# Stick-breaking attention in a two-layer decoder trunk: another order of units, masks, read-outs and conversions

## The chip, the cores and the metric

The kernel runs on one core of one Trainium2 chip. The metric is device time in microseconds: the median of 3 runs is 1889.95 us (1888.29 to 1889.99). The profile comes from one further execution.

## The reference, cut to what matters

Two layers work on 512 tokens of width 2048, in fp32. The first is a sparse attention layer and isn't touched. The second is stick-breaking attention over keys and values of 4 groups, with 16 query heads of 128 (4 heads to a group):

```python
z = einsum('bqngd,bsnd->bngqs', qg, k) * HEAD_DIM ** -0.5
strict = key_pos[None, :] < t[:, None]
log_om = where(strict, -softplus(z), 0.0)
suffix = cumsum(log_om, reverse=True) - log_om       # over the keys
a = where(strict, exp(log_sigmoid(z) + suffix), 0.0)
o = einsum('bngqs,bsnd->bqngd', a, v)
...
return (o * silu(gate)) @ w_o                         # gate = x @ w_in[:, WIDTH_B:]
```

So each query sums softplus over the keys between a key and itself, from the latest key backwards, and the sum has to go from one block of 128 keys to the next earlier one.

## The kernel before, in words

All matrices are laid out features by tokens, in tiles of 128 by 512. Every fp32 product is three fp32r matmuls (mm3, L135 to L138) of high and low halves; `split` (L131 to L133) makes the halves: a copy on ACT (hi) and a subtraction on DVE (lo). The weights come through SP's DMA queue, and each 128 x 512 piece is split into wh and wl (`plain_items`, L232).

**The stage.** For each of 4 head groups g (loop at L1357) PE computes the gate projection for 4 blocks of 128 columns into banks 0 to 3 (64 steps of one mm3, `gemm_w`, L289; for group 0 `gate_first`, L1214), and between its steps the attention of the group in 10 units. A unit (i, kb) is query block i (4 heads x 128 queries = 512 columns) against key block kb <= i (128 rows). The class `Sticks` (L1240) has its steps:

- `logits` (L1252): mm3 of keys and queries into a bank z (4 + u % 2; bank 7 for unit 0). On a diagonal unit (kb == i) DVE adds the mask (z<-z,gone). ACT does Abs (wk<-z), Exp and Ln (wk<-wk); DVE joins max(z, 0) and the logarithm into softplus (wk<-z,wk): "the sum" in the prediction.
- `parts` (L1268): for kb < i DVE adds the total that the later key block left (wk<-wk,t or wk<-t,ident,wk); DVE makes the halves sh and sl. For kb > 0 ACT copies a row or 32 rows of z into a tile t.
- `weights` (L1287): two matmuls (L1291) of a triangle of -1 with sh and sl onto z; ACT takes the exponential (wk<-z); for kb > 0 DVE subtracts z from t (t<-t,z), which is the total for unit (i, kb - 1): "the read-out". Then the halves of the result, hi on ACT and lo on DVE (c<-wk).
- `values` (L1303): three matmuls (L1310 to L1312) with the values onto bank 6 or 7 (o); after a row's last unit ACT copies it to F (f<-o).

Units stand in the order of L1244: a row's units run from its diagonal to kb = 0, always two places apart, so the total has a turn's time. The diagonals are units 0, 1, 7 and 8.

**The order.** `turn` (L1321) for s = 1 to 11 issues on PE: logits of s, one gate step, values of s - 2, one gate step, weights of s - 1, then three gate steps (fewer for some turns of group 0). The rest of `logits` and of `parts` for unit s follows where these are called. PE keeps this order as written. On ACT and DVE the compiler of the kernel schedules by its own model of time (L1432); what runs under `paced` (L325) is held behind the instruction of its engine that was written just before it. A weight conversion is not held so, nor is a SiLU, so a held instruction written right after one of them hangs on that one alone and may move with it.

**Conversions.** Queries lie in F and are scaled and split for each row i by `split_scaled` (L1208: c<-f on ACT and on DVE), into Q[i], once the previous group has finished with row i (L1336: after turns 8, 9 and 11 the rows 2, 3 and 0; L1373: row 1 at the end of the group). `split_keys` (L1164: c<-E) converts a group's keys. They wait in the list `bg`, and `pumped` (L339) takes one from it at each gate step (at every second one in group 0).

**Between groups** (L1370 to L1377): when the gate is done, ACT takes its SiLU from banks 0 to 3 (wk<-g) and DVE multiplies the result into F. The next group then loads ACT's table for Exp and Ln (L1359), issues the logits of units 0 and 1 (`begin`, L1316), and 11 gate steps before turn 1. Group 0 starts beside its own gate (L1345 to L1355).

Of the kernel before, what the change touches and what calls it, by code (L numbers as in the profile page):

```python
# [10 lines left out]
F32 = mybir.dt.float32  # L11
# [66 lines left out]
def trunk_kernel(  # L78
# [85 lines left out]
    units = []  # L164
# [1075 lines left out]
    class Sticks:  # L1240

        units = [(3, 3), (2, 2), (3, 2), (2, 1), (3, 1), (2, 0), (3, 0), (1, 1), (0, 0), (1, 0)]  # L1244

        def __init__(self, g):
# [3 lines left out]
            self.out = {}  # L1250

        def logits(self, u):  # L1252
            i, kb = self.units[u]
            z = bank(4 + u % 2 if u else 7, "z")
            ks = slice(kb * 128, (kb + 1) * 128)
            mm3(z, [k[:, ks] for k in K[self.g]], Q[i], True, True)
            e = work()
            sp = work()
            if kb == i:
                v = z.rearrange("p (h q) -> p h q", h=4)  # L1260
                dve.tensor_tensor(v, v, gone[i % 2].unsqueeze(1).broadcast_to([128, 4, 128]), ALU.add)
            act.activation(e, z, AF.Abs)
            act.activation(e, e, AF.Exp, scale=-1.0)
            act.activation(e, e, AF.Ln, bias=1.0)
            dve.scalar_tensor_tensor(sp, z, 0.0, e, ALU.max, ALU.add)
            self.state[u] = z, sp

        def parts(self, u):  # L1268
# [9 lines left out]
            hi, lo = (px.tile([128, 512], F32R, name=f"s{s}", tag=f"s{s}", bufs=2) for s in "hl")  # L1278
            dve.tensor_copy(hi, sp)
            dve.tensor_tensor(lo, sp, hi.bitcast(F32), ALU.subtract)  # L1280
            if kb:
                rows = slice(96, 128) if kb % 2 else slice(0, 1)
                self.total[i, kb] = px.tile([128, 512], F32, name="t", tag="t", bufs=3)
                act.activation(self.total[i, kb][rows], z[rows], AF.Copy)
            self.state[u] = z, hi, lo

        def weights(self, u):  # L1287
# [6 lines left out]
            if kb:  # L1294

                rows = slice(96, 128) if kb % 2 else slice(0, 1)
                total = self.total[i] = self.total.pop((i, kb))
                dve.tensor_tensor(total[rows], total[rows], z[rows], ALU.subtract)
            hi, lo = A[u % 2]
            split(hi, lo, a)  # L1300
            self.state[u] = hi, lo

        def values(self, u):  # L1303
# [7 lines left out]
            pe.matmul(o, vl, hi, start=False, stop=False)  # L1311
            pe.matmul(o, vh, lo, start=False, stop=kb == 0)  # L1312
            if kb == 0:
                act.activation(F[self.g][:, :, i * 128 : (i + 1) * 128], o.rearrange("p (h q) -> p h q", h=4), AF.Copy)
# [40 lines left out]
    gemm = pumped(chunk, 2)  # L1355

    for g in range(4):  # L1357
        if g:
            log_exp()  # L1359
            banks = mm_banks("g")  # L1360
            gemm = pumped(gemm_w(items, plain, banks))
            sticks = Sticks(g)
            sticks.begin(0)
            sticks.begin(1)
        if 0 < g < 3:
            bg.append(lambda g=g: split_keys(g + 1))
        steps(gemm, 11 if g else 0)
        for s in range(1, 12):
# [67 lines left out]
```

## Time and profile before

| | |
|---|---|
| median of 3 runs | 1889.95 us |
| the profiled execution | 1889.72 us, span 1888.0 us |
| PE, matmuls | 1865.0 us busy (99%), 9181 instructions |
| PEld, weight loads | 1577.3 us (84%) |
| DVE | 1235.1 us (65%) |
| ACT | 938.6 us (50%) |
| DMA | 189.21 MB, mean 100 GB/s |
| the chain that ended last | PE 94%, DVE 3%, ACT 2%, issue 1% |

Times are microseconds from the start of the span. A row of the timeline gives start, duration, engine, line, operation, out<-in by the program's names (buffer numbers left out: c is any of the tiles for halves of keys, queries, values and results), the shape, and in brackets the engine's idle time before it with what ended that. All helpers' instructions have line 111. A matmul of 128 x 512 is shown 0.39 long, but they overlap: what counts is the distance between starts. The four groups lie about at 1240 to 1324, 1391, 1459 and 1511 us.

### The profile page before, as it was taken

The page shows a single profiled execution, that of the slowest core. Times are in us where ns is not written, and L with a number is a line of the kernel's source. Part 1 is how long each engine was busy: PE and PEld are TensorE (multiplying, and loading weights), DVE is VectorE, ACT ScalarE, POOL GpSimd, SP SyncE. Part 2 cuts the span into 40 slices and gives each one's busy share as a digit, 9 for nine tenths or more (in the row PEclk, how much of TensorE's full clock was granted, in tenths as well). Part 3 has the DMA queues.
Part 4 walks back from the last instruction along what each step waited for, and adds up shares of the span by engine and source line. Part 5 has one row for each costly group of instructions (what it writes and reads, how often), then busy time and mean ns, then how long its engine had stood idle before and what let it go on. Part 6 is the DMA issues. An engine that isn't in the chain of part 4 may idle for free.

```text
span 1888.0 us, 24839 instructions
## 1 busy us (share of the span) xinstructions
PE 1865.0 (99%) x9181; PEld 1577.3 (84%) x9181; DVE 1235.1 (65%) x2395; ACT 938.6 (50%) x1696; POOL 4.7 (0%) x20
## 2 busy tenths in 40 slices
PE   9999999999999999999999999998999999999998
PEld 8898888888888888888888999976777788888887
DVE  5768678567565455675377888876877745567534
ACT  3546423455554433474245444477777643347422
POOL 0000000000000000000000000000000000000000
PEclk9999999999999999999999999999999999999999
DMA  6442333312221522433343333322222162242333
GB/s 195 126 123 62 95 101 90 101 56 68 78 67 57 189 90 79 126 98 122 101 146 112 101 102 110 104 78 68 63 62 65 57 189 92 79 131 91 123 101 112
DMA packets 111178, 189.21 MB, mean 100 GB/s; under 512 B 8528, under 2 KB 29008, under 8 KB 111056
## 3 DMA queue, kind: packets, MB, share of 16 engines
q1 hardware_dynamic: 111056, 187.62, 32.8%
q8 instruction: 72, 1.18, 0.3%
q14 instruction: 50, 0.41, 0.1%
HBM read 179.21 MB, written 8.39 MB: 99 GB/s over the span
## 4 chain that ended last, share of the span: by engine, by line
PE 94%; DVE 3%; ACT 2%; issue 1%; DMA 0%; SPq 0%; ACTq 0%; DVEq 0%
PE g L136 11%; PE g L137 11%; PE g L138 11%; PE o L138 7%; PE o L136 7%; PE o L137 7%; PE m L136 4%; PE m L138 4%; PE m L137 4%; PE q L136 3%; PE q L138 3%; PE q L137 3%; PE k L137 2%; PE k L138 2%; PE k L136 2%; ACT wk L111 1%
## 5 line engine op out<-in xcount | busy, mean ns | idle before, releaser
L111 ACT ACTIVATE wh<-raw 128x512 fp32r<-128x512 f32 (+3 forms) x685 | 397.8, 582 | 699.5 <-PE g L137 231.1
L111 DVE TENSOR_TENSOR wl<-raw,wh 128x512 fp32r<-128x512 f32 (+3 forms) x685 | 430.6, 629 | 461.6 <-ACT wh L111 446.2
L136 PE MATMUL g<-xh,wh 128*128 128x512 f32 x1024 | 405.0, 396 | 0.0
L137 PE MATMUL g<-xl,wh 128*128 128x512 f32 x1024 | 400.6, 391 | 0.0
L138 PE MATMUL g<-xh,wl 128*128 128x512 f32 x1024 | 400.6, 391 | 0.0
L138 PEld LDWEIGHTS g<-xh,wl 128*128 128x128 f32 x1024 | 192.9, 188 | 41.4
L137 PEld LDWEIGHTS g<-xl,wh 128*128 128x128 f32 x1024 | 193.2, 189 | 37.5
L136 PEld LDWEIGHTS g<-xh,wh 128*128 128x128 f32 x1024 | 193.1, 189 | 37.3 <-issue 0.3
L138 PE MATMUL o<-xh,wl 128*128 128x512 f32 x512 | 199.3, 389 | 0.0
L136 PE MATMUL o<-xh,wh 128*128 128x512 f32 x512 | 199.2, 389 | 0.0
L137 PE MATMUL o<-xl,wh 128*128 128x512 f32 x512 | 199.2, 389 | 0.0
L138 PEld LDWEIGHTS o<-xh,wl 128*128 128x128 f32 x512 | 96.1, 188 | 20.4 <-DVE wl L111 0.3
L137 PEld LDWEIGHTS o<-xl,wh 128*128 128x128 f32 x512 | 96.1, 188 | 20.0
L136 PEld LDWEIGHTS o<-xh,wh 128*128 128x128 f32 x512 | 96.1, 188 | 19.8
L136 PE MATMUL q<-xh,wh 128*128 128x512 f32 x256 | 99.6, 389 | 0.0
L137 PE MATMUL q<-xl,wh 128*128 128x512 f32 x256 | 99.6, 389 | 0.0
L138 PE MATMUL q<-xh,wl 128*128 128x512 f32 x256 | 99.6, 389 | 0.0
L111 ACT ACTIVATE sh<-st 128x512 fp32r<-128x512 f32 x80 | 49.7, 624 | 44.4 <-DVE st L111 44.3
L111 ACT ACTIVATE wk<-z 128x512 f32<-128x512 f32 x80 | 47.2, 594 | 42.1 <-PE z L138 15.7
L111 DVE TENSOR_TENSOR sl<-st,sh 128x512 fp32r<-128x512 f32 x80 | 55.1, 690 | 13.9 <-ACT sh L111 13.9
L111 DVE TENSOR_TENSOR xl<-f,xh 128x512 fp32r<-128x512 f32 x80 | 54.4, 687 | 12.6 <-ACT f L111 12.3
L138 PEld LDWEIGHTS q<-xh,wl 128*128 128x128 f32 x256 | 48.0, 188 | 10.1
(287 smaller groups left out, 3323.7 us busy)
## 6 DMA issues: line engine op xcount, KB each, us to landing
raw<-w_in_a SPq DMA_DIRECT2D x95, 512.0 KB, 3.7
raw<-w_in_b SPq DMA_DIRECT2D x64, 512.0 KB, 3.8
raw<-w_ple_gate SPq DMA_DIRECT2D x52, 512.0 KB, 3.7
raw<-w_o_a SPq DMA_DIRECT2D x24, 512.0 KB, 3.7
raw<-w_o_b SPq DMA_DIRECT2D x24, 512.0 KB, 3.8
raw<-w_kv_b SPq DMA_DIRECT2D x16, 512.0 KB, 3.8
raw<-w_ple_gate SPq DMA_DIRECT2D x24, 256.0 KB, 2.9
f<-xT SPq DMA_DIRECT2D x4, 1024.0 KB, 6.3
```

Of the source, the lines that this page charges most:

```text
L111: ins = method(*args, **kw)
L136: pe.matmul(out, a[0], b[0], start=start, stop=False)
L137: pe.matmul(out, a[0], b[1], start=False, stop=False)
L138: pe.matmul(out, a[1], b[0], start=False, stop=stop)
```

## The change

The units take another order, so that the diagonals are units 0, 1, 5 and 8, still with a row's units two places apart. `logits`, `parts` and `weights` are cut into smaller steps: `logits` (matmuls and mask), `soft` (Abs, Exp, Ln), `plus` (the sum), `high` (total, sh, copy to t), `low` (sl), `weights` (matmuls, exponential, read-out), `halves` (hi and lo of the result), `values`, and `leave` (f<-o). In the turn of a diagonal unit `low` of the unit before goes behind the mask, and `plus` behind the read-out of the unit before; `leave` always goes behind the turn's other work. The first logits and masks of a group are written ahead of the previous group's SiLUs, the rest of both units (`begin`) behind them; 12 gate steps follow instead of 11. Row 2 of the queries and the next group's keys are converted behind those 12 steps, row 1 already after turn 5 (group 0: turn 8).

```diff
-        units = [(3, 3), (2, 2), (3, 2), (2, 1), (3, 1), (2, 0), (3, 0), (1, 1), (0, 0), (1, 0)]
+        units = [(3, 3), (1, 1), (3, 2), (1, 0), (3, 1), (2, 2), (3, 0), (2, 1), (0, 0), (2, 0)]
...
+        def diagonal(self, u):
+            return u < 10 and self.units[u][0] == self.units[u][1]
...
         def begin(self, u):
-            paced(self.logits, u)
-            if u == 0:
-                paced(self.parts, u)
+            for fn in (self.soft, self.plus, self.high, self.low):
+                paced(fn, u)
 
         def turn(self, s, gemm, gaps):
 
+            late = self.diagonal(s)
             if 1 < s < 10:
                 paced(self.logits, s)
+                if late:
+                    paced(self.low, s - 1)
+                paced(self.soft, s)
+                if not late:
+                    paced(self.plus, s)
             steps(gemm, gaps[0])
             if s > 1:
                 paced(self.values, s - 2)
             steps(gemm, gaps[1])
             if s < 11:
                 paced(self.weights, s - 1)
-                if s < 10:
-                    paced(self.parts, s)
+                if 1 < s < 10 and late:
+                    paced(self.plus, s)
+                paced(self.halves, s - 1)
+                if 1 < s < 10:
+                    paced(self.high, s)
+                    if not self.diagonal(s + 1):
+                        paced(self.low, s)
+            if s > 1:
+                paced(self.leave, s - 2)
             steps(gemm, gaps[2])
-            if self.g < 3 and s > 6:
-
-                bg.extend(lambda i=i: split_scaled(self.g + 1, i) for i in {8: (2,), 9: (3,), 11: (0,)}.get(s, ()))
+
+            if self.g < 3:
+                bg.extend(lambda i=i: split_scaled(self.g + 1, i) for i in QUERIES_DONE[self.g > 0].get(s, ()))
+
+    QUERIES_DONE = {8: (1,), 9: (3,), 11: (0,)}, {5: (1,), 9: (3,), 11: (0,)}
...
-    bg.extend(lambda i=i: after_combining(split_scaled, 0, i) for i in (3, 2))
+    bg.extend(lambda i=i: after_combining(split_scaled, 0, i) for i in (3, 1))
...
-    steps(gemm, 9)
-    sticks.begin(0)
-    steps(gemm, 1)
-    sticks.begin(1)
-    bg.extend(lambda i=i: split_scaled(0, i) for i in (1, 0))
+    for u, n in enumerate((9, 1)):
+        steps(gemm, n)
+        paced(sticks.logits, u)
+    for u in range(2):
+        sticks.begin(u)
+    bg.extend(lambda i=i: split_scaled(0, i) for i in (2, 0))
     steps(gemm, 8)
     gemm = pumped(chunk, 2)
 
     for g in range(4):
         if g:
-            log_exp()
-            banks = mm_banks("g")
-            gemm = pumped(gemm_w(items, plain, banks))
-            sticks = Sticks(g)
-            sticks.begin(0)
-            sticks.begin(1)
+            steps(gemm, 12)
+            bg.append(lambda g=g: split_scaled(g, 2))
         if 0 < g < 3:
             bg.append(lambda g=g: split_keys(g + 1))
-        steps(gemm, 11 if g else 0)
...
         run(gemm)
         drain()
         if g < 3:
-            bg.append(lambda g=g: split_scaled(g + 1, 1))
+            then = Sticks(g + 1)
+            for u in range(2):
+                paced(then.logits, u)
         for h in range(4):
             sg = work()
             act.activation(sg, banks[h], AF.Silu)
             dve.tensor_tensor(F[g][:, h], F[g][:, h], sg, ALU.mult)
+        if g < 3:
+            sticks = then
+            log_exp()
+            for u in range(2):
+                sticks.begin(u)
+            banks = mm_banks("g")
+            gemm = pumped(gemm_w(items, plain, banks))
```

More of the change, by code (lines that the diff above doesn't have):

```diff
@@ L1250, in __init__, with totals @@
             self.out = {}
+        def diagonal(self, u):
+            return u < 10 and self.units[u][0] == self.units[u][1]
+        def totals(self, kb):
+            return slice(96, 128) if kb % 2 else slice(0, 1)
         def logits(self, u):
             i, kb = self.units[u]
-            z = bank(4 + u % 2 if u else 7, "z")
+            z = self.state[u] = bank(4 + u % 2 if u else 7, "z")
             ks = slice(kb * 128, (kb + 1) * 128)
             mm3(z, [k[:, ks] for k in K[self.g]], Q[i], True, True)
-            e = work()
-            sp = work()
             if kb == i:
@@ L1264, in logits, with plus, high @@
             act.activation(e, e, AF.Ln, bias=1.0)
+            self.state[u] = z, e
+        def plus(self, u):
+            z, e = self.state[u]
+            sp = work()
             dve.scalar_tensor_tensor(sp, z, 0.0, e, ALU.max, ALU.add)
             self.state[u] = z, sp
-        def parts(self, u):
+        def high(self, u):
             i, kb = self.units[u]
@@ L1277, in parts, with low @@
                     dve.scalar_tensor_tensor(sp[rows], total[rows], ident[rows, 127:128], sp[rows], ALU.mult, ALU.add)
-            hi, lo = (px.tile([128, 512], F32R, name=f"s{s}", tag=f"s{s}", bufs=2) for s in "hl")
+            hi = px.tile([128, 512], F32R, name="sh", tag="sh", bufs=2)
             dve.tensor_copy(hi, sp)
-            dve.tensor_tensor(lo, sp, hi.bitcast(F32), ALU.subtract)
             if kb:
-                rows = slice(96, 128) if kb % 2 else slice(0, 1)
+                rows = self.totals(kb)
                 self.total[i, kb] = px.tile([128, 512], F32, name="t", tag="t", bufs=3)
                 act.activation(self.total[i, kb][rows], z[rows], AF.Copy)
+            self.state[u] = z, sp, hi
+        def low(self, u):
+            z, sp, hi = self.state[u]
+            lo = px.tile([128, 512], F32R, name="sl", tag="sl", bufs=2)
+            dve.tensor_tensor(lo, sp, hi.bitcast(F32), ALU.subtract)
             self.state[u] = z, hi, lo
@@ L1294, in weights, with halves @@
             if kb:
-                rows = slice(96, 128) if kb % 2 else slice(0, 1)
+                rows = self.totals(kb)
                 total = self.total[i] = self.total.pop((i, kb))
                 dve.tensor_tensor(total[rows], total[rows], z[rows], ALU.subtract)
-            hi, lo = A[u % 2]
-            split(hi, lo, a)
-            self.state[u] = hi, lo
+            self.state[u] = a
+        def halves(self, u):
+            a = self.state[u]
+            self.state[u] = A[u % 2]
+            split(*A[u % 2], a)
         def values(self, u):
```

8 lines of the change are left out of this document (7 added, 1 removed).

## The prediction

> **What bounds the kernel now.** I read the page first: PE is busy all along and its rows are the longest in the chain that ended last, so the time is the matmuls plus whatever keeps PE from the next one. The profiled execution took 1889.72 us, 1.7 us of it outside the span below; the three timed runs have a median of 1889.95 us, 0.01% away, so what I take off the profiled execution holds for the median too.
>
> ```profile
> span 1888.0 us, 24839 instructions
> ```
>
> The change touches only the stick-breaking stage, so next I asked for the busy times in stretches: four stretches that follow the head groups 0 to 3, then three short ones in which the matmuls came further apart. Columns: stretch, its length, then each engine's busy time with its instructions, the granted clock (PEclk), DMA.
>
> ```profile
> 1239.20:1324.30 85.10, 77.29 (x310) 59.31 (x309) 63.22 (x108) 63.60 (x113) 0.00 (x0) 0.96 0.25 74
> 1324.30:1391.20 66.90, 64.06 (x273) 50.34 (x272) 50.81 (x81) 51.39 (x88) 0.00 (x0) 1.00 0.21 63
> 1391.20:1458.90 67.70, 64.03 (x273) 50.40 (x272) 51.36 (x82) 51.66 (x89) 0.00 (x0) 1.00 0.21 62
> 1458.90:1511.00 52.10, 50.03 (x211) 40.26 (x211) 37.49 (x60) 36.62 (x62) 0.00 (x0) 0.97 0.18 52
> 1253.80:1257.20 3.40, 3.40 (x9) 2.63 (x8) 1.70 (x3) 1.55 (x3) 0.00 (x0) 0.51 0.36 125
> 1294.90:1298.10 3.20, 3.20 (x9) 2.51 (x8) 1.30 (x2) 1.73 (x3) 0.00 (x0) 0.50 0.18 67
> 1496.30:1499.60 3.30, 3.30 (x9) 2.58 (x8) 1.71 (x4) 1.86 (x3) 0.00 (x0) 0.52 0.02 5
> ```
>
> The reader should count matmuls here, not busy time. Undisturbed, they start 0.2267 us apart (below, 1423.61 to 1425.65: nine steps in 2.04 us). The four stretches hold 310, 273, 273 and 211, worth 70.3, 61.9, 61.9 and 47.8 us, and take 85.1, 66.9, 67.7 and 52.1: **14.8 + 5.0 + 5.8 + 4.3 = 29.9 us are lost**. That is the ceiling of what a new order can win. The short stretches ran at half the clock: 27 matmuls took 9.9 us in place of 6.1, so 3.8 of the 29.9 are these dips.
>
> Last the waits of PE in the stage (waiting engine, tile, line <- who ended it: us in total, times, longest):
>
> ```profile
> PE z L136 <- DVE t L111: 9.0, 5, 2.5
> PE o L1310 <- ACT c L111: 2.6, 4, 1.0
> PE z L1291 <- DVE sl L111: 2.5, 8, 0.7
> PE z L1291 <- DVE sh L111: 1.5, 2, 1.1
> PE o L1312 <- DVE c L111: 0.5, 1, 0.5
> ```
>
> They sum to 16.1 us idle. The loss beyond the dips is 29.9 - 3.8 = 26.1 us: after each wait the next few matmuls start further apart too. So I price **an idle microsecond at 26.1 / 16.1 = 1.62 us**.
>
> **The change part by part.** Nothing is added or removed in sum: the same matmuls, masks, conversions and table loads. All of it is order, on PE, ACT and DVE; no moved step issues a DMA, so SP's and POOL's queues stay as they are.
>
> *Read-outs ahead of the sum (row one, 9.0 us).* The logits of a unit overwrite the bank of the unit two before; that is free once DVE has read the total out of it (t). Four of the five waits are unit 9's, one per group. Here it is in group 2: DVE, ACT, PE, from the start of unit 8, a diagonal one.
>
> ```profile
> 1421.41 0.42 DVE L111 CAST sh<-wk 128x512 fp32r<-128x512 f32 x1
> 1422.08 0.69 DVE L111 TENSOR_TENSOR wl<-raw,wh 128x512 fp32r<-128x512 f32 x1 [0.25 <-ACT wh L111]
> 1422.69 0.68 DVE L111 TENSOR_TENSOR sl<-wk,sh 128x512 fp32r<-128x512 f32 x1
> 1423.29 0.69 DVE L111 TENSOR_TENSOR z<-z,gone 128x512 f32<-128x512 f32 x1
> ...
> 1426.44 0.68 DVE L111 SCALAR_TENSOR_TENSOR wk<-z,wk 128x512 f32<-128x512 f32 x1
> 1427.16 0.69 DVE L111 TENSOR_TENSOR t<-t,z 32x512 f32<-32x512 f32 x1
> ```
>
> ```profile
> 1424.02 0.60 ACT L111 ACTIVATE wk<-z 128x512 f32<-128x512 f32 x1 [0.53 <-DVE z L111]
> 1424.65 0.63 ACT L111 ACTIVATE wk<-wk 128x512 f32<-128x512 f32 x1
> 1425.19 0.62 ACT L111 ACTIVATE wh<-raw 128x512 fp32r<-128x512 f32 x1
> 1425.71 0.61 ACT L111 ACTIVATE wk<-wk 128x512 f32<-128x512 f32 x1
> 1426.23 0.58 ACT L111 ACTIVATE wk<-z 128x512 f32<-128x512 f32 x1
> ```
>
> ```profile
> 1421.11 0.39 PE L138 MATMUL z<-c 128*128 128x512 f32 x1
> ...
> 1423.61 0.39 PE L1291 MATMUL z<-sl,down 128*128 128x512 f32 x1
> ...
> 1425.65 0.39 PE L138 MATMUL g<-xh,wl 128*128 128x512 f32 x1
> 1427.91 0.50 PE L136 MATMUL z<-c,c 128*128 128x512 f32 x1 [1.87 <-DVE t L111]
> ```
>
> Unit 8's logits end at 1421.50, but its mask (z<-z,gone) starts only at 1423.29, behind sl. ACT's Abs, Exp and Ln follow, with a weight conversion (wh) between, and only then unit 7's exponential (1426.23); DVE then does the sum (1426.44) and the read-out t (1427.16). Unit 9 was due at 1425.88 and starts at 1427.91.
>
> The change does two things here. The read-out goes ahead of the sum: worth only 0.32 us, since the exponential ends at 1426.81 and t could start at 1426.84. And low, which makes sl, goes behind the mask: the mask can then start at the end of sh, 1421.87, instead of 1423.29. With the same steps after it: mask to 1422.56, Abs from 1422.6 to 1423.2, Exp to 1423.85, wh 0.52, Ln to 1425.0, the exponential to 1425.6, t to 1426.33. Unit 9 would wait **0.45 us instead of 1.87**. Behind the mask on DVE now stands sl, and for that PE's weights matmul waits: sl runs from 1422.59 to 1423.27, wl behind it, before the matmul at 1423.61.
>
> But the new order of units has a price. Before, the later diagonals are units 7 and 8; unit 6, ahead of the first of them, is (3, 0) and passes on no total, so only one read-out stands in a diagonal unit's turn. After, they are units 5 and 8, and both follow units, (3, 1) and (2, 1), that pass one on. So there are eight such turns in the stage, not four. Each waits from 0 (no weight conversion between: 0.52 earlier) to 1.65 us (mask still behind wl and sl: t from 1426.84 to 1427.53). I take 0.45, from the chain just worked out: 8 x 0.45 = 3.6 us idle. 9.0 becomes 3.6 and, at 1.62, **14.6 becomes 5.8**.
>
> *First logits and masks ahead of the SiLUs (rows two and five, 3.1 us).* The step from group 1 to 2, ACT, DVE, PE:
>
> ```profile
> 1377.76 0.64 ACT L111 ACTIVATE c<-f 128x512 fp32r<-128x512 f32 x1
> 1378.28 0.64 ACT L111 ACTIVATE c<-E 128x512 fp32r<-128x512 f32 x1
> ...
> 1381.37 0.60 ACT L111 ACTIVATE wk<-z 128x512 f32<-128x512 f32 x1
> ```
>
> ```profile
> 1385.60 0.69 DVE L111 TENSOR_TENSOR z<-z,gone 128x512 f32<-128x512 f32 x1
> ```
>
> ```profile
> 1385.74 0.50 PE L1291 MATMUL z<-sl,down 128*128 128x512 f32 x1 [0.16 <-DVE sl L111]
> ...
> 1390.17 0.50 PE L1310 MATMUL o<-c,c 128*128 128x512 f32 x1 [0.54 <-ACT c L111]
> ```
>
> Two conversions (of the queries, c<-f, and of the keys, c<-E) run ahead of the last SiLU, and unit 1's mask comes at 1385.60, so its whole ACT chain lands on the half that the values matmul at 1390.17 waits for. After, both masks follow the group's first logits directly. Without the two conversions ACT starts on unit 0 some 1.04 us earlier (two steps of 0.52), and unit 1 follows without waiting for a mask. Against 0.54 us idle that is enough at all three steps between groups. PE's own cover stays: one gate step of three matmuls (0.68 us) moves from the end of a group to behind its successor's first logits. What is late next is the SiLU of the banks that the new group's gate matmuls overwrite; now it has 0.68 us less. The SiLUs' products stand behind the masks on DVE, which wait for six matmuls of PE at most (1.36 us), and only the next layer's output gemm, far off, reads them.
>
> At the start of group 0 there is no SiLU, and two conversions of queries stand ahead of unit 0's halves as before; its waits, 1.0 + 0.5 us, may go or stay, and low of unit 1 now goes ahead of them. I keep half, 0.8 us: **5.0 becomes 1.3**, bounds 0 and 5.0.
>
> *Conversions for later behind (rows three and four, 4.0 us).* Group 2's last diagonal is followed by two conversions of queries on DVE:
>
> ```profile
> 1431.48 0.68 DVE L111 SCALAR_TENSOR_TENSOR c<-f,c 128x512 fp32r<-128x512 f32 x1
> ...
> 1433.17 0.69 DVE L111 SCALAR_TENSOR_TENSOR c<-f,c 128x512 fp32r<-128x512 f32 x1
> ```
>
> They stand ahead of unit 9's halves, and its weights wait. After, groups 1 and 2 keep one of them there; row 2's goes behind the next group's opening, with the keys, which gives back 0.69 us; row 1's, so far at the step between groups, goes to turn 6. There it delays a read-out by 0.69 unless the logits of unit 6 on ACT cover it; DVE has no total to add for diagonal unit 5, which is room of the same size. Group 0 keeps two and group 3 has none; the other waits of these rows come from group 0's middle, where the restored activations are split as well, and the change takes nothing off that. So half, 2.0 us idle: **6.5 becomes 3.2**; bounds 0 and, if low behind the mask comes late in all eight diagonal turns by the 0.7 us that is row three's longest, 4.0 + 5.6 = 9.6 us idle. The totals' copies, the buffers (six work tiles, two pairs of halves) and leave, which goes behind the exponential, I cost at nothing: each new holder is done a whole turn, 23 matmuls or 5.2 us, before its successor comes.
>
> *Dips (3.8 us).* Two of the three start right behind waits of row one that the change shortens:
>
> ```profile
> 1293.77 0.50 PE L136 MATMUL z<-c,c 128*128 128x512 f32 x1 [2.54 <-DVE t L111]
> ```
>
> ```profile
> 1495.64 0.50 PE L136 MATMUL z<-c 128*128 128x512 f32 x1 [1.87 <-DVE t L111]
> ```
>
> The first dip follows group 0's opening waits. I let the two go and half of the first stay: **3.8 becomes 0.7**. The wait at 1427.91, as long as that at 1495.64, was followed by none, so this term is a matter of timing. [...]
>
> **Sum.** Loss after: 5.8 + 1.3 + 3.2 + 0.7 = 11.0 us; saved 29.9 - 11.0 = 18.9; 1889.72 - 18.9 = 1870.8, so **1871 us**.
>
> **The rivals.**
>
> *Everything hides (0.16): 1863.* No weight conversion falls into the eight turns (0), the boundaries are clean, rows three and four halve again (1.6) and the opening of group 0 keeps 1.3: 2.9 us of loss stay, 27 saved. For it: ACT and DVE are busy 51 of 67 us per group. Against it: ACT makes a weight conversion every four gate steps, more than one per turn.
>
> *Half a gain (0.18): 1879.* ACT and DVE keep only the order in which an instruction hangs on the one written just before it; weight conversions and SiLUs hang on nothing, so what follows one may drift with it. The rows show it: c<-f and c<-E of 1377.76 are written behind the Abs of 1381.37 and run ahead. If the mask drifts so that a diagonal turn waits 1.0 us: 13.0 + 1.3 + 3.2 + two dips 2.5 = 20.0 stay, 10 saved.
>
> *The dips stay though the waits go (0.05): 1874*, 3.1 us above the forecast. For it, the wait without a dip; against it, their places.
>
> *The change doesn't do what it says (0.04): 1890.* The mask drifts behind sl as now, 1.65 us in eight turns: 21.4, with 1.3, 3.2 and three dips 3.8 that is 29.7 of the 29.9.
>
> *Slower (0.13): 1900.* The diagonal turn itself. Sum, halves and low of both units now stand behind the mask and the read-out on one queue; if the mask also comes behind a conversion pair (the one moved next to unit 5, or those of groups 0 and 1 next to unit 8), a turn waits 1.65 + 0.69 = 2.34 us, eight times: 30.3, and with twice as many such waits four dips (5.0), with 1.3 and 3.2: 39.8, 10 us slower. It decides from (29.9 - 5.2) / (8 x 1.62) = 1.9 us per diagonal turn. For it: there are now eight such turns, and group 0's middle has DVE and ACT busy 63 of 85 us; against it: 1.9 is as long as the present wait, and both causes of that one are cut.
>
> **How the numbers follow.** Forecast 0.44 (1866 to 1874), and the rivals as given. This kernel's measurement tells about 0.2%, 3.8 us, from no change. Faster: 0.44 + 0.16 + 0.18 + 0.05 = 0.83; same 0.04; slower 0.13. The range goes from the rival in which everything hides to a little beyond half a gain, 1862 to 1884, and leaves the last two cases out.
>
> **What would show it.** PE's row "z <- DVE t" shrinks from 9.0 us in 5 waits to about 3.6 in eight or fewer; the masks of units 5 and 8 start within 0.5 us of their logits' end or right behind sh, and t runs ahead of the sum. Between groups both masks run before or among the SiLUs, "o <- ACT c" is left with group 0's wait alone, and the stretch of groups 1 and 2 takes 63 to 64 us instead of 66.9 and 67.7 (their floor is 61.9). The granted clock stays 1.00 from group 1 on. Wrong would be: a mask behind sl, waits of the gate matmuls for a SiLU, or group 0 as long as before, since half of the loss lies in its 85 us.

## The result, and the profile after

The changed kernel takes **1879.6 us** (median of 4 runs, 1879.21 to 1879.76) against 1889.77 us for the kernel before (median of 4, 1888.29 to 1889.99): a ratio of 0.9948, 95% interval 0.993 to 0.9965. That is faster by 10.2 us, and inside the predicted range, but 8.6 us above the forecast of 1871. It is the time of the rival "half a gain" (1879). The profiled execution took 1879.65 us, 1.75 of it outside the span.

```profile
span 1877.9 us, 24827 instructions
```

The same four stretches follow, one per head group (length; busy time and instructions of PE, PEld, DVE, ACT, POOL; granted clock; DMA).

```profile
1239.20:1321.50 82.30, 75.47 (x319) 58.67 (x318) 64.91 (x110) 64.21 (x114) 0.00 (x0) 1.00 0.25 77
1321.50:1387.00 65.50, 63.53 (x272) 50.02 (x271) 50.34 (x81) 51.11 (x87) 0.00 (x0) 1.00 0.21 65
1387.00:1453.20 66.20, 64.28 (x275) 50.70 (x274) 51.08 (x83) 51.61 (x88) 0.00 (x0) 1.00 0.21 64
1453.20:1501.00 47.80, 47.22 (x204) 37.42 (x203) 34.90 (x56) 35.21 (x59) 0.00 (x0) 1.00 0.19 57
```

Count matmuls again, at 0.2267 us each. The stretches are worth 72.3, 61.7, 62.3 and 46.2 us, so 10.0 + 3.8 + 3.9 + 1.6 = **19.3 us are still lost, where it was 29.9**. The 10.6 us between them are the whole gain (1889.72 - 1879.65 = 10.1); nothing outside this stage moved the time. The clock is 1.00 in all four, so the dips are gone. The waits of PE in the stage:

```profile
PE z L136 <- DVE t L111: 5.5, 8, 1.6
PE o L1334 <- DVE c L111: 2.4, 3, 0.8
PE z L1310 <- DVE sl L111: 1.8, 6, 0.6
PE z L1310 <- DVE sh L111: 1.5, 3, 1.1
```

11.2 us idle, against 16.1. One idle microsecond costs 19.3 / 11.2 = 1.72 us. The row "z <- DVE t" went from 9.0 to 5.5, but its eight waits are not the eight that I forecast. Unit 9's wait (1.87 to 2.54 before) is gone from all four groups. Row "o <- ACT c" (2.6) is gone, and a row "o <- DVE c" of nearly the same size stands in its place.

**A diagonal turn that works.** Unit 5 in group 1: DVE, ACT, PE.

```profile
1335.06 0.68 DVE L111 TENSOR_TENSOR z<-z,gone 128x512 f32<-128x512 f32 x1
1335.66 0.41 DVE L111 CAST sh<-wk 128x512 fp32r<-128x512 f32 x1
1336.10 0.69 DVE L111 TENSOR_TENSOR sl<-wk,sh 128x512 fp32r<-128x512 f32 x1
...
1338.97 0.69 DVE L111 TENSOR_TENSOR t<-t,z 32x512 f32<-32x512 f32 x1 [0.98 <-ACT wk L111]
1339.69 0.69 DVE L111 SCALAR_TENSOR_TENSOR wk<-z,wk 128x512 f32<-128x512 f32 x1
```

```profile
1335.78 0.60 ACT L111 ACTIVATE wk<-z 128x512 f32<-128x512 f32 x1 [1.42 <-DVE z L111]
1336.63 0.63 ACT L111 ACTIVATE wh<-raw 128x512 fp32r<-128x512 f32 x1 [0.26 <-PE g L137]
1337.17 1.28 ACT L111 ACTIVATE wk<-wk 128x512 f32<-128x512 f32 x2
1338.36 0.58 ACT L111 ACTIVATE wk<-z 128x512 f32<-128x512 f32 x1
```

```profile
1339.72 0.50 PE L136 MATMUL z<-c 128*128 128x512 f32 x1 [0.31 <-DVE t L111]
```

The mask runs even ahead of sh, a weight conversion stands among the three steps on ACT as supposed (between Abs and Exp, where it was between Exp and Ln), and the read-out goes ahead of the sum. The wait is 0.31 us; 0.45 was forecast.

**Where the wait went.** The step from group 1 to 2 (DVE, then PE):

```profile
1382.50 0.69 DVE L111 TENSOR_TENSOR sl<-wk,sh 128x512 fp32r<-128x512 f32 x1
1383.10 0.69 DVE L111 SCALAR_TENSOR_TENSOR c<-f,c 128x512 fp32r<-128x512 f32 x1
1383.70 0.69 DVE L111 TENSOR_TENSOR c<-E,c 128x512 fp32r<-128x512 f32 x1
1384.42 0.69 DVE L111 TENSOR_TENSOR t<-t,z 32x512 f32<-32x512 f32 x1
1385.14 0.69 DVE L111 TENSOR_TENSOR c<-wk,c 128x512 fp32r<-128x512 f32 x1
```

```profile
1385.89 0.50 PE L1334 MATMUL o<-c,c 128*128 128x512 f32 x1 [0.84 <-DVE c L111]
```

The two conversions that were moved behind the opening now stand on DVE ahead of unit 0's read-out and low half (c<-wk,c), and PE waits for that half. The ACT exponential was over at 1383.60. At the step to group 3, which has no keys to convert, one conversion and sl of unit 1 stand there, and the wait is 0.75 us.

In group 0 two query conversions come ahead of unit 2's sum, but there they hold it up on ACT (first fence), where they stand ahead of unit 2's Abs. DVE is idle for 0.54 us ahead of the sum (second fence), so their halves on DVE are not what it waits for:

```profile
1250.93 1.16 ACT L111 ACTIVATE c<-f 128x512 fp32r<-128x512 f32 x2
1252.11 0.60 ACT L111 ACTIVATE wk<-z 128x512 f32<-128x512 f32 x1
```

```profile
1254.07 0.69 DVE L111 SCALAR_TENSOR_TENSOR wk<-z,wk 128x512 f32<-128x512 f32 x1 [0.54 <-ACT wk L111]
...
1255.85 0.69 DVE L111 TENSOR_TENSOR t<-t,z 32x512 f32<-32x512 f32 x1
```

```profile
1256.60 0.50 PE L136 MATMUL z<-c,c 128*128 128x512 f32 x1 [1.60 <-DVE t L111]
```

This wait, the longest of the stage now, is in no diagonal turn: it is unit 3's.

### The profile page after: what moved, and what is told of

It is laid out like the page before. It is cut to its first block, busy times and chain, and to the rows that moved or that the text cites. A ratio compares the mean times of both kernels' runs of the same rounds, so it can differ in the third digit from the quotient of the medians.

```text
span 1877.9 us, 24827 instructions
## 1 busy us (share of the span) xinstructions
PE 1860.1 (99%) x9181; PEld 1573.8 (84%) x9181; DVE 1233.5 (66%) x2395; ACT 938.0 (50%) x1696; POOL 4.7 (0%) x20
## 4 chain that ended last, share of the span: by engine, by line
PE 96%; DVE 2%; ACT 1%; issue 0%; DMA 0%; SPq 0%; DVEq 0%
PE g L136 12%; PE g L137 12%; PE g L138 12%; PE o L138 7%; PE o L137 7%; PE o L136 7%; PE m L136 4%; PE m L138 4%; PE m L137 4%; PE q L136 3%; PE q L138 3%; PE q L137 3%; PE k L137 2%; PE k L138 2%; PE k L136 2%; PE iq L138 1%
## 5 line engine op out<-in xcount | busy, mean ns | idle before, releaser
L138 PEld LDWEIGHTS q<-xh,wl 128*128 128x128 f32 x256 | 48.0, 188 | 10.1
```

What stands on the lines that cost most here:

```text
L138: pe.matmul(out, a[1], b[0], start=False, stop=stop)
```

## The experiments

None of the twelve kernels leaves anything out of the work. "Loss" is the sum over 1236 to 1512 us of what PE's starts lie further apart than 0.2267 us; by that count before loses 30.9 us and after 20.9. The medians of before in their batches were 1889.36 to 1889.77 us. The letters in the quoted expectations name theories: A, the order of units costs time and the new turns pay it back, against B, it costs nothing; C, the moved conversions make the new waits and a better place ends them, against D, DVE is nearly full and they pay elsewhere; E to I are told where they come up.

| kernel | median us (runs from, to) | ratio to before, 95% | loss us |
|---|---|---|---|
| order_alone | 1894.4 (1892.17 to 1896.97) | 1.0029, 1.0016 to 1.0041 | 34.8 |
| plain_eleven | 1891.23 (1889.88 to 1893.27) | 1.0009, 0.9999 to 1.0018 | 32.6 |
| plain_turns | 1884.57 (1882.82 to 1886.0) | 0.9972, 0.9962 to 0.9983 | 26.2 |
| begin_old | 1882.22 (1881.77 to 1883.43) | 0.9966, 0.9953 to 0.9978 | 23.1 |
| low_ahead | 1881.12 (1880.87 to 1881.37) | 0.9958, 0.9946 to 0.9971 | 22.2 |
| sum_ahead | 1880.74 (1880.38 to 1880.87) | 0.9956, 0.9943 to 0.997 | 21.8 |
| masks_behind | 1879.63 (1879.36 to 1879.79) | 0.995, 0.9938 to 0.9963 | 20.8 |
| first_late | 1879.29 (1878.9 to 1880.12) | 0.9949, 0.9936 to 0.9961 | 20.6 |
| row3_late | 1878.39 (1878.02 to 1878.63) | 0.9943, 0.9931 to 0.9956 | 19.7 |
| conv_spread | 1878.24 (1877.88 to 1878.7) | 0.9942, 0.9929 to 0.9954 | 19.5 |
| old_order | 1875.89 (1875.49 to 1876.09) | 0.9929, 0.9916 to 0.9941 | 17.2 |
| best_old | 1872.58 (1872.38 to 1872.74) | 0.9913, 0.9899 to 0.9926 | 13.8 |

### Does the order of units cost time?

**order_alone** is the kernel before with the new order of units and nothing else; the rows of queries follow the units.

```diff
-        units = [(3, 3), (2, 2), (3, 2), (2, 1), (3, 1), (2, 0), (3, 0), (1, 1), (0, 0), (1, 0)]
+        units = [(3, 3), (1, 1), (3, 2), (1, 0), (3, 1), (2, 2), (3, 0), (2, 1), (0, 0), (2, 0)]
...
-                bg.extend(lambda i=i: split_scaled(self.g + 1, i) for i in {8: (2,), 9: (3,), 11: (0,)}.get(s, ()))
+                bg.extend(lambda i=i: split_scaled(self.g + 1, i) for i in {8: (1,), 9: (3,), 11: (0,)}.get(s, ()))
...
```

> The kernel before with the new order of units alone (and the rows of the queries converted in the order that it needs). Theory A, the prediction's: the order by itself costs, since both later diagonal turns now have a read-out to wait for and the mask still comes behind sl; eight waits of about 1.65 us instead of four of 1.87 to 2.54, so 1892 to 1898 us. Theory B: it is the order that gives the gain, since diagonals no longer follow one another and the sum of one no longer stands right ahead of the read-out of the other: 1880 to 1885 us, with PE's waits for t under 6 us.

1894.4 us, 4.9 above before in its batch: A. The waits of its stage:

```profile
PE z L136 <- DVE t L111: 13.1, 9, 3.0
PE o L1310 <- ACT c L111: 2.6, 4, 1.0
```

The row of the read-outs has nine waits instead of five and 13.1 us instead of 9.0. In groups 1 to 3 unit 9's wait stays at 1.87 and 0.77 to 0.80 us behind unit 5 come on top, half of the 1.65 that was expected there. The boundary row is that of before, 2.6 in 4.

**old_order** is the reverse: the kernel after with the old order of units.

```diff
-        units = [(3, 3), (1, 1), (3, 2), (1, 0), (3, 1), (2, 2), (3, 0), (2, 1), (0, 0), (2, 0)]
+        units = [(3, 3), (2, 2), (3, 2), (2, 1), (3, 1), (2, 0), (3, 0), (1, 1), (0, 0), (1, 0)]
...
-    QUERIES_DONE = {8: (1,), 9: (3,), 11: (0,)}, {5: (1,), 9: (3,), 11: (0,)}
+    QUERIES_DONE = {8: (2,), 9: (3,), 11: (0,)}, {7: (2,), 9: (3,), 11: (0,)}
...
-            bg.append(lambda g=g: split_scaled(g, 2))
+            bg.append(lambda g=g: split_scaled(g, 1))
...
```

> The kernel after with the old order of units (diagonals 7 and 8), all else kept. Theory A: the cure of the diagonal turn works on four waits instead of eight, so it is as fast or faster than after, 1875 to 1880 us. Theory B: two diagonals in a row load DVE and ACT with two masks and leave unit 9 late; unit 9's wait stays over 1 us per group and the time is 1884 to 1889 us.

1875.89 us, 3.7 below after: A again. Its read-out row is 3.7 us in 4 waits, for 5.5 in 8:

```profile
PE z L136 <- DVE t L111: 3.7, 4, 1.5
```

Both ways round the new order of units costs 4 to 5 us. (In old_order one conversion moves with it, in groups 1 and 2 from behind turn 5 to behind turn 7, so its 3.7 us are not of the order alone.) The whole gain of the change, and some more, is in the rest of it.

### What in the diagonal turn pays?

**plain_turns** is the kernel after whose diagonal turns are like all others: sum ahead of the read-out, low in its own turn.

```diff
-            late = self.diagonal(s)
+            late = False
...
-                    if not self.diagonal(s + 1):
+                    if True:
                         paced(self.low, s)
```

> The kernel after with diagonal turns issued like all others (sl of the unit before ahead of the mask, the sum ahead of the read-out). Theory A: the mask falls back behind sl, a diagonal turn waits 1.2 us longer, eight times: 1889 to 1896 us. Theory B: the mask hangs on a weight conversion anyway and has drifted ahead, so only the sum's place counts: 1880 to 1883 us.

1884.57 us, 5.0 above after: between the two ranges, so neither theory had the size. The waits show why. In groups 1 to 3 each of the two diagonal turns waits only 0.56 to 0.60 us (a loss of 0.73 to 0.76), not 1.5 or more. Most of the cost is group 0's unit 9: it waits 2.6 us. The mean granted clock of the span is 0.999, where after has 1.000.

```profile
PE z L136 <- DVE t L111: 9.6, 10, 2.6
```

DVE in group 1 shows that unit 8's mask runs ahead of sh and sl although nothing in the code asks for that any more:

```profile
1355.31 0.69 DVE L111 TENSOR_TENSOR wl<-raw,wh 128x512 fp32r<-128x512 f32 x1
1355.91 0.69 DVE L111 TENSOR_TENSOR z<-z,gone 128x512 f32<-128x512 f32 x1
1356.52 0.42 DVE L111 CAST sh<-wk 128x512 fp32r<-128x512 f32 x1
1356.97 0.69 DVE L111 TENSOR_TENSOR sl<-wk,sh 128x512 fp32r<-128x512 f32 x1
```

**plain_eleven** is plain_turns with 11 gate steps ahead of turn 1 instead of 12, and asks whether that is due to the count. A weight conversion is written every four steps. It is held behind nothing, and what is written next is held behind it alone.

```diff
-            steps(gemm, 12)
+            steps(gemm, 11)
```

> The kernel is the one of plain_turns with 11 instead of 12 gate steps ahead of turn 1 in groups 1 to 3; nothing is left out. Theory I: with 12 steps the weight conversion that comes every four steps is written last in turn 7, directly ahead of unit 8's mask, so that the mask, which is held only behind the instruction written just before it, hangs on a conversion that nothing holds and drifts ahead of unit 8's last SiLU product; with 11 steps it hangs on that product again, as in the kernel before. Then the mask stands behind sl in groups 1 to 3, the logits behind the read-out of unit 9 wait 1.7 to 2.0 us there instead of 0.74, and the time is 1887 to 1889 us. Rival: the mask's place does not depend on the count, or does not set the wait; the time stays at 1884 to 1885 us and the wait at 0.74.

The mask is behind sl again, and the wait is that of before to the hundredth:

```profile
1355.63 0.69 DVE L111 TENSOR_TENSOR sl<-wk,sh 128x512 fp32r<-128x512 f32 x1
1356.24 0.69 DVE L111 TENSOR_TENSOR z<-z,gone 128x512 f32<-128x512 f32 x1
...
1360.33 0.69 DVE L111 TENSOR_TENSOR t<-t,z 32x512 f32<-32x512 f32 x1
```

```profile
1361.08 0.50 PE L136 MATMUL z<-c 128*128 128x512 f32 x1 [1.87 <-DVE t L111]
...
1428.50 0.50 PE L136 MATMUL z<-c,c 128*128 128x512 f32 x1 [1.87 <-DVE t L111]
...
1497.16 0.54 PE L136 MATMUL z<-c 128*128 128x512 f32 x1 [1.87 <-DVE t L111]
```

So the count of gate steps, 11 or 12, decides where unit 8's mask stands, as theory I has it; that it does so through the conversion written just ahead of the mask is read from the code. The time, 1891.23 us, lies above both ranges. Three waits of 1.87 us lose 2.03 each at their first matmul, where 0.58 lost 0.74: 3.9 us of the 6.4 by which the loss rises from plain_turns. Half clock behind two of the three costs another 3.1 us, which I had left out; other waits are 0.6 us shorter in sum. Of the rows below, the last two show the second of these waits: the 3.41 us ahead of the half clock, and the half clock itself, from 1429.22. The first two lie 68.27 us earlier, 20 times 3.413, and show the first wait:

```profile
1357.54:1360.95 3.41, 1.67 (x8) 1.05 (x6) 1.91 (x3) 3.23 (x7) 0.00 (x0) 1.00 0.20 76
1360.95:1364.37 3.42, 3.29 (x14) 2.74 (x15) 2.12 (x5) 2.04 (x4) 0.00 (x0) 1.00 0.00 0
1425.81:1429.22 3.41, 1.54 (x7) 0.99 (x6) 2.73 (x5) 2.70 (x5) 0.00 (x0) 1.00 0.01 3
1429.22:1432.63 3.41, 3.41 (x10) 2.64 (x9) 1.67 (x3) 1.86 (x3) 0.00 (x0) 0.50 0.00 0
```

The waits are equally long, but the first goes 0.13 us beyond the end of its stretch and full clock follows, while the second lies inside and half clock follows. The third is like the second (granted clock 0.56 from 1497.10 to 1500.50).

The next two take the halves of the diagonal turn apart. **sum_ahead** puts only the sum back ahead of the read-out:

```diff
-                if not late:
-                    paced(self.plus, s)
+                paced(self.plus, s)
...
-                if 1 < s < 10 and late:
-                    paced(self.plus, s)
```

> The kernel after with one half of the diagonal turn undone: the sum stands ahead of the values and so of the read-out again, sl stays behind the mask. Both halves undone cost 5 us (1884.6). Theory A, the prediction's (mask 1.42 us, sum 0.32 us of unit 9's wait): the smaller part, 1880.5 to 1881.5 us. Rival G: the mask drifts ahead of sl anyway, so the sum's place is nearly all of it, 1883 to 1884.6 us, with waits of 0.7 us at the logits behind both diagonal units.

1880.74 us, 1.1 above after; the time is A's, but the waits are on the side of the rival G: 0.54 to 0.58 us (0.71 to 0.74 lost) behind both diagonal units in groups 1 to 3, where after has 0.31 to 0.33 behind unit 5 and none behind unit 8. The total is small because unit 7 waits less in exchange: nothing instead of 0.39 and 0.41 us in groups 1 and 2, and 0.32 instead of 0.85 in group 0, with every conversion where it was. So the late sum has a part in those waits. **low_ahead** puts only low back into its own turn:

```diff
-                if late:
-                    paced(self.low, s - 1)
...
-                    if not self.diagonal(s + 1):
-                        paced(self.low, s)
+                    paced(self.low, s)
```

> The kernel after with the other half undone: sl of the unit before stands ahead of the mask again, the sum stays behind the read-out. Theory A: the larger part of the 5 us, 1883 to 1884.6 us. Rival G: 1879 to 1881 us.

1881.12 us, 1.5 above after, between the ranges. Groups 1 to 3 are like those of after: the mask drifts ahead there in any case. The cost is all in group 0, where the mask of unit 8 does fall behind sl (it starts 2.37 us after its logits' end instead of 0.95) and "o <- DVE c" gains a fourth wait of 1.2 us. Alone the halves are worth 1.1 and 1.5 us, together 5.0. With either half in place group 0's unit 9 is in time; without both it waits 2.6 us.

### What is the opening worth?

**masks_behind** writes a group's first logits and masks behind the SiLUs and the table load (theory E: their place ahead of them is worth nothing).

```diff
         if g < 3:
             then = Sticks(g + 1)
-            for u in range(2):
-                paced(then.logits, u)
...
         if g < 3:
             sticks = then
             log_exp()
+            for u in range(2):
+                paced(then.logits, u)
```

> The kernel after with a group's first logits and masks written behind the previous group's SiLUs, as before (both units' logits still ahead of the rest of either). Theory E: what helps between groups is that unit 1's mask no longer stands behind unit 0's halves, not that both stand ahead of the SiLUs, since PE's 36 gate matmuls leave more than 1 us there: no difference, 1879 to 1880.5 us. Rival: the prediction's, the place ahead of the SiLUs counts: a wait of weights or values of 0.5 to 1 us comes back per group, 1882 to 1884 us.

1879.63 us, as after: E. **begin_old** keeps the new places of the conversions but opens a group as before, unit 0 whole, unit 1 only to its sum, and unit 1's halves in turn 1 (F: that brings the old boundary waits back; H: it doesn't matter).

```diff
-            for fn in (self.soft, self.plus, self.high, self.low):
+            for fn in (self.logits, self.soft, self.plus, self.high, self.low)[: 3 if u else 5]:
                 paced(fn, u)
...
-                if 1 < s < 10:
+                if s < 10:
                     paced(self.high, s)
...
```

> The kernel after with a group opened as before: unit 0's logits, mask, ACT chain, sum and halves, then unit 1's logits, mask, chain and sum, and unit 1's halves in turn 1; all behind the SiLUs. Theory F: opening both units' masks at once is the other large part of the gain beside the diagonal turns (group 0's opening lost 4.0 us before and none after, and its dip went with it): 1883 to 1886 us, with waits for ACT's half at the first values. Rival H: the conversions, which no longer stand ahead of the first exponential, did that, and the openings stay as they are: 1879 to 1881 us.

1882.22 us, 2.6 above after, between the ranges. The old row is back with more than its old size,

```profile
PE o L1332 <- ACT c L111: 3.2, 4, 1.0
```

and in exchange the waits for DVE fall ("o <- DVE c" to 0.7, the 1.6 of group 0's unit 3 is gone), which is why it costs less than F gave.

### Do the moved conversions make the new waits?

**conv_spread** puts row 2 of the queries behind turn 2, the keys behind turn 3 and row 1 behind turn 6.

```diff
-    QUERIES_DONE = {8: (1,), 9: (3,), 11: (0,)}, {5: (1,), 9: (3,), 11: (0,)}
+    QUERIES_DONE = {8: (1,), 9: (3,), 11: (0,)}, {6: (1,), 9: (3,), 11: (0,)}
...
-            bg.append(lambda g=g: split_scaled(g, 2))
-        if 0 < g < 3:
-            bg.append(lambda g=g: split_keys(g + 1))
         for s in range(1, 12):
             sticks.turn(s, gemm, (0 if s == 1 else 1, 1 if s > 1 else 0, 2 if s == 10 or not g and s % 2 else 3))
+            if g and s == 2:
+                bg.append(lambda g=g: split_scaled(g, 2))
+            if 0 < g < 3 and s == 3:
+                bg.append(lambda g=g: split_keys(g + 1))
```

> The kernel after with the two conversions behind a group's opening put later and apart (queries of row 2 after turn 2, keys after turn 3), and row 1's queries one turn later (after turn 6). Theory C: the 0.8 us for which PE's third values matmul of unit 0 now waits in groups 1 to 3 is the two conversions that stand on DVE ahead of unit 0's lower half; it goes (three times 1.0 to 1.1 us), as does the wait of unit 7 for a read-out in groups 1 and 2 (0.55 each): 1875 to 1877 us. Rival D: DVE is full there, and the waits only move to the turns that take the conversions: 1879 to 1881 us.

1878.24 us, 1.4 below after, between C and D.

```profile
PE z L136 <- DVE t L111: 4.8, 6, 1.6
PE z L1310 <- DVE sl L111: 2.8, 11, 0.6
PE z L1310 <- DVE sh L111: 1.5, 3, 1.1
PE o L1334 <- DVE c L111: 0.2, 1, 0.2
```

The boundary waits fall from 2.4 to 0.2 and the read-out waits by 0.7: so these conversions made them. But 1.0 us comes back in eleven waits for sl, where after has six: unit 2's weights in groups 1 to 3, now behind row 2's conversion, and unit 6's in groups 1 and 2, behind row 1's.

**first_late** does the same in group 0 alone: rows 2 and 0 behind turns 2 and 5 instead of at the opening.

```diff
-    bg.extend(lambda i=i: split_scaled(0, i) for i in (2, 0))
...
+            if not g and s in (2, 5):
+                paced(split_scaled, 0, {2: 2, 5: 0}[s])
```

> The kernel after with group 0's own two conversions of queries (rows 2 and 0) put behind turns 2 and 5. Theory C: the 1.6 us that unit 3 of group 0 waits for unit 1's read-out is these two, which stand on DVE ahead of the sum of unit 2; it goes, with its restart 1.9 us: 1877 to 1878.5 us, unless turns 3 and 6, where they land, wait in turn. Rival D: group 0's first turns are full on DVE, the wait moves to units 4 to 7: 1879 to 1881 us.

1879.29 us, no gain to speak of: D. Unit 3's wait of 1.6 us is gone, so the conversions made it. Unit 6's grew from 1.31 to 1.79, with row 0's conversion now on ACT ahead of unit 5's Exp, and half clock came with it: the granted clock is 0.54 from 1272.80 to 1276.20.

```profile
1272.83 0.64 PE L136 MATMUL z<-c,c 128*128 128x512 f32 x1 [1.79 <-DVE t L111]
```

**row3_late** releases row 3 after turn 10 instead of 9, away from unit 9's weights.

```diff
-    QUERIES_DONE = {8: (1,), 9: (3,), 11: (0,)}, {5: (1,), 9: (3,), 11: (0,)}
+    QUERIES_DONE = {8: (1,), 10: (3,), 11: (0,)}, {5: (1,), 10: (3,), 11: (0,)}
```

> The kernel after with row 3 of the next group's queries converted after turn 10 instead of turn 9. Theory C: unit 9's weights wait in groups 0 to 2 (about 1.0, 0.9 and 0.9 us with restarts of 0.1) for this one conversion of 0.69 us on DVE; most of it goes, 0.7 to 0.9 us per group: 1877 to 1878 us. Rival D: it then stands ahead of the SiLUs on ACT and the next group's gate matmuls wait: 1879.5 to 1881 us.

1878.39 us, 1.2 below after, between C and D. Unit 9's weights lose 0.51 instead of 0.97 us in groups 1 and 2, "z <- DVE sh" falls from 1.5 to 0.5, and a new wait of 0.5 us for f comes up between groups 0 and 1.

**best_old** puts it together: old_order, with all its conversions given places of their own.

```diff
-    QUERIES_DONE = {8: (2,), 9: (3,), 11: (0,)}, {7: (2,), 9: (3,), 11: (0,)}
+    QUERIES_DONE = {9: (2,), 10: (3,), 11: (0,)}, {5: (2,), 10: (3,), 11: (0,)}
...
-    bg.extend(lambda i=i: split_scaled(0, i) for i in (1, 0))
...
-            bg.append(lambda g=g: split_scaled(g, 1))
-        if 0 < g < 3:
-            bg.append(lambda g=g: split_keys(g + 1))
         for s in range(1, 12):
             sticks.turn(s, gemm, (0 if s == 1 else 1, 1 if s > 1 else 0, 2 if s == 10 or not g and s % 2 else 3))
+            if not g and s in (3, 5):
+                paced(split_scaled, 0, {3: 1, 5: 0}[s])
+            if g and s == 2:
+                bg.append(lambda g=g: split_scaled(g, 1))
+            if 0 < g < 3 and s == 3:
+                bg.append(lambda g=g: split_keys(g + 1))
```

> The kernel after with the old order of units and the conversions apart: a group's row 1 after turn 2, keys after turn 3, next group's row 2 after turn 5 (group 0: 9), row 3 after turn 10, group 0's own two after turns 3 and 5. Old order alone gave 1875.9. Theory C: three waits of unit 0's values (1.0 to 1.2 each), unit 9's weights in three groups (0.9 each), unit 3's logits in group 0 (1.7) and unit 9's logits in two groups (0.9 each) lose their cause, 9 us in all, and about half comes back elsewhere: 1869 to 1873 us. Rival D: DVE is full, all of it moves: 1875 to 1877 us.

1872.58 us, 0.9913 of before, in C's range: it beats both kernels, after by 7.0 us.

```profile
PE z L1310 <- DVE sl L111: 2.5, 8, 0.7
PE z L136 <- DVE t L111: 1.4, 1, 1.4
PE z L1310 <- DVE sh L111: 1.1, 1, 1.1
PE z L136 <- ACT f L111: 0.5, 1, 0.5
PE o L1334 <- DVE c L111: 0.2, 1, 0.2
```

5.7 us idle, for 11.2 after: one wait for a read-out is left, in group 0, and the largest row that remains is sl's.

## Why the prediction was right, and where it was wrong

**Right: the sign, the stage and the ceiling.** The time came out of the 29.9 us of spacing in this stage and out of nothing else. That the time is the one of the rival "half a gain" is luck: the rival had 13.0 us in row one from a drifting mask and 2.5 us of dips, and measured are 9.5 us in that row, more than half of it behind units that are no diagonal, and no dip. One sign was missed: the stretches of groups 1 and 2 take 65.5 and 66.2 us, not 63 to 64.

**Right in direction, and the failed step: "Conversions for later behind".** I priced the move of the conversions as a relief of 2.0 us idle on rows three and four, and of the boundaries I said that the earlier start on ACT "is enough at all three steps between groups". Neither is so. At the boundaries the conversions stand on DVE ahead of a read-out or a low half, and PE waits 2.4 us there (forecast 0). In group 0, whose two conversions keep their place in the code, they now run on ACT ahead of unit 2's Abs, and unit 3 waits 1.6 us. Unit 7 waits 0.39 and 0.41 us in groups 1 and 2: this is the delay of 0.69 that I named and thought covered. Rows three and four came to 3.3 us, not 2.0. first_late and conv_spread show the cause, since these waits go when the conversions are moved. At unit 7 it is one of two causes: sum_ahead leaves the conversion and the wait goes all the same. The sum behind the read-out uses up the room that I had counted on: in group 1 unit 6's Abs comes 1.67 us after its first matmul in after (1339.72 to 1341.39) and 1.01 us in sum_ahead. In the same way the 0.85 us of group 0's unit 7 fall to 0.32 with the sum ahead; the key conversion that stands ahead of that read-out was not moved in any run. A better place alone gives little with the new order of units, 0.3 to 1.4 us: the wait comes back at the next tight unit.

The sum by terms, idle us: row one 5.5 for 3.6, rows two and five 2.4 for 0.8 (all of it new, the opening of group 0 has none), rows three and four 3.3 for 2.0. At 1.72 us that is 9.5 + 4.1 + 5.7 = 19.3 us, for 11.0 forecast with the dips. The 8.3 us between them are nearly the whole error of 8.6.

**Row one, by its own chain.** In the part that comes from diagonal turns the forecast was on the careful side: 3.6 us idle in eight turns; the waits behind unit 5 are 1.31, 0.31, 0.33 and 0.33 us and behind unit 8 none, 2.3 in all. So the sum of this part is near, but not as eight waits of 0.45: more than half of it is group 0's unit 6 alone. That the new order of units costs by itself is as forecast, and now has a size: 4.9 us from before, 3.7 from after. Its two halves: the sum behind the read-out was given 0.32 us a turn; sum_ahead against after shows 0.21 to 0.25 behind unit 5 and 0.55 to 0.58 behind unit 8. The mask ahead of sl was given 1.42; plain_eleven against plain_turns shows 1.29 (1.87 to 0.58). Both are near, except that the sum's place is worth more behind unit 8 than was given; in groups 1 to 3 the waits that they leave are shorter than the 0.45 of the chain. And in those groups it is not the line `low` behind the mask that brings this for unit 8: the twelfth gate step alone lets the mask drift ahead (plain_turns), and the eleventh undoes it (plain_eleven). The rival "half a gain" had this drift as a loss; here it was a gain.

**"First logits and masks ahead of the SiLUs".** Their place is worth nothing (masks_behind). What cures the old boundary is that both units are opened together and that unit 1's halves don't wait for turn 1: 2.6 us (begin_old).

**Dips.** 0.7 us was forecast to stay, none did; the longest wait is now 1.60 us. That the dips hang on the waits is borne out: in the experiments they come back behind waits of 1.79 (first_late, granted clock 0.54 over 3.40 us), 2.66 (plain_eleven, 0.76 over 3.30) and two of three of 1.87 us (plain_eleven, 0.61 and 0.56 over 3.40), and in order_alone behind group 0's opening (waits of 1.03 and 0.54, clock 0.52 over 3.20) and its wait of 3.0 (0.52 over 3.10). The rival "the dips stay" is out.

**Open.** No theory gave the sizes of plain_turns, plain_eleven, low_ahead, begin_old, conv_spread and row3_late. Each undoes several waits that share a queue, and a wait that goes makes the next one late. How the 5.0 us of the two halves together divide up was not tried beyond group 0's unit 9. Nor was the new order of units tried with all conversions placed as in best_old, nor the kernel after with 11 gate steps: whether the line `low` would there do in groups 1 to 3 what the twelfth step does is open.

## What to carry to other kernels

Before an instruction is moved "behind", look at what comes next at the new place, on each engine that has a part of it: DVE is busy 65 of 82 us in group 0, and a conversion of 0.69 us that leaves one wait is the next one, unless it goes into a turn with room. When an order is only partly held, a count that seems to have nothing to do with it (11 or 12 steps) can decide it, so read the order from the trace, not from the code. Try the parts of a change one by one: here one part (the order of units) cost 4 us that the others paid for.

## What the runs showed of the hardware

In the stage of before the granted clock is 0.50 in three stretches of 3.41 us (1253.71 to 1257.12, 1294.67 to 1298.08, 1496.06 to 1499.47) and 1.00 between them. Matmuls start 0.43 us apart in them (1496.31 to 1499.30: seven steps in 2.99 us), where 0.2267 is usual. Each of the three stands behind waits of PE: 1.03 and 0.54 us at the opening of group 0, 2.54 us up to 1293.77, and 1.87 us up to 1495.64. The starts of the three are 40.96 and 201.39 us apart, 12 and 59 times 3.413.

But half clock does not follow each wait. In before and in plain_eleven there are three waits of 1.87 us each. Half clock follows the one that ends at 1495.64 in before and those that end at 1428.50 and 1497.16 in plain_eleven. It does not follow those that end at 1360.94 and 1427.91 in before (granted clock 1.00 from 1427.90 to 1431.30) and at 1361.08 in plain_eleven (1.00 from 1360.95 to 1364.37). Count steps of 3.413 us from a half clock of the same trace: the first three waits lie each inside one step, and the other three go across the end of one, with at most 1.75 us on one side. Group 0's opening has waits of 1.03 and 0.54 us in order_alone and in begin_old alike; the granted clock behind them is 0.52 in the first (1255.10 to 1258.30) and 1.00 in the second (1253.30 to 1256.70). The wait of 1.60 us in after is followed by full clock (1.00 from 1256.60 to 1260.00), the one of 1.79 in first_late by half clock (0.54 from 1272.80 to 1276.20). So in these traces the length of a wait alone does not tell whether half clock follows, which cost 3.1 us behind two of the three waits of plain_eleven. What decides it was not shown: no run moved a wait by itself.

After a wait without a dip PE also loses more than the idle time: 2.03 us at the first matmul and 0.11 at the second for a wait of 1.87 (before, 1427.91). So in this stage the waits cost more than their sum: it lost 1.62 us (before, without the dips) and 1.72 us (after) for each idle microsecond listed.
